# A fifteenth pair of chunks by seven products in layer 1's first MLP product, the two ordinary chunks at its head

## Chip, cores and metric

The kernel runs on one core of one Trainium2 chip. The metric is the device time of one execution in microseconds; three runs were made, and their median counts. Less is better.

## What is computed

The reference is a trunk of two layers over two sequences of 512 tokens with 1024 features, in float32. Layer 0 mixes tokens by a Fourier transform, layer 1 by attention; each is followed by the same MLP.

```python
def sq_relu_mlp(h, w_up, w_down):
    a = jnp.maximum(h @ w_up, 0)
    return (a * a) @ w_down

def trunk(x, ...):
    for i in range(DEPTH):
        ...
        x = x + sq_relu_mlp(rms_norm(x, mlp_norm[i]), mlp_w_up[i], mlp_w_down[i])
    return rms_norm(x, final_norm)
```

The inner width D_FF is 4096. The change touches the first of the two MLP products, `h @ w_up`, of layer 1.

## The kernel before

**Numbers.** Every float32 operand is split into two parts of a format that TensorE takes at full pace (`split`, L82 and L83: ScalarE casts the high part, VectorE subtracts to get the low part). A product of 128 x 128 x 512 is three matmuls.

**First product.** The 4096 columns of `w_up` are 32 chunks of 128. The operand h is cut in four blocks: its first and second half of features, for each of the two sequences (`b11`, `b21` for sequence 0, `b12`, `b22` for sequence 1). Two chunks together form a pair, and a pair is a 2 x 2 block product (chunks by sequences). It is computed by seven block products instead of eight (the scheme of Strassen and Winograd), with sums of weights (`sums_13`, `sum_2`, `sum_4`) and sums of operands (`t1` to `t4`). Each block product is `product` (L863): four blocks of 128 features, three matmuls each, so twelve matmuls of 512 columns. `Pair.first` and `Pair.second` issue two of the seven, `Pair.rest` the other five.

Layer 0 takes all 32 chunks as 16 pairs (`NPS = (16, 14)`). Layer 1 takes 14 pairs, and the chunks 28 to 31 in the ordinary way (`Regular`): per chunk and sequence two block products, 24 matmuls.

**What becomes of the results.** After the squared ReLU a pair's four results are combined by `Pair.out` (four subtractions on GpSimd, for the last pair on VectorE) and stored to DRAM (`spill`) as seven operands of the second product, which also multiplies blocks by seven products. The operands go in groups (`ROW_GROUPS`, `SUM_GROUPS`): in layer 1 the first group of `b11` and `b21` holds pairs 0 to 3, the first group of `t1`, `t3`, `t2`, `b22`, `t4` pairs 0 and 1. The results of the ordinary chunks go to `plain` in DRAM and are read at the very end of the layer, in a product with the rest of `w_down`.

**Order in layer 1, before.** `first_product` runs, in program order: `first` and `second` of the first six pairs (`AHEADS[1]` is 6), while `blocks.second()` prepares the operands of sequence 1 and the sums step by step (`next(todo)`); the four ordinary chunks for sequence 1 (L1070); `rest` of the pairs 0 to 12, with `first` of the later pairs; `rest` of pair 13; the four ordinary chunks for sequence 0 (L1119). During the last `rest` a generator, `ahead`, fetches and splits the first operands of the second product: it is resumed at three places of `rest` (L963, L970, L977), and drained after it.

**Order in layer 0.** There the last pair's `first` and `second` are issued inside the `rest` of the last but one (`early`), which frees the buffers of `b11` and `b21` sooner, and `ahead` is resumed once before that, three times in it, and three times in the last `rest`. Each resumption fetches one operand and splits the one fetched in the step before.

**Second product.** `second_product` (L1122) begins in layer 1 with one row block (`Row`, twelve matmuls per half, from `b11` and later `b21`), and between its halves and after them the five products of `Sums` with `t1`, `t3`, `t2`, `b22`, `t4`. In the first group each of these five is six matmuls. Their weights are sums again (`sum_123`, `sum_4`), made on VectorE from two loads (`w_sum`) and split (`split_12`, `split_3`, `split_4`).

**Who sets the order.** A list scheduler places the instructions on each engine by program order and readiness, also ahead of earlier ones that are not ready; each engine then executes its own list in order. Under `tc.manual_schedule(engines=...)` the instructions of the named engines keep their program order among each other. Buffers come from pools: 38 buffers of 4 KB a partition (`act`) of which the blocks of h take 28 in the first product, five for raw weights, four for split weights, eight PSUM banks. A load waits until a buffer is free. SP issues most DMAs, ScalarE's queue the stores of `b11`, `b21`, `b22` and `plain`.

Of the kernel before, what the change touches and what calls it, by code (L numbers as in the profile page):

```python
# [18 lines left out]
P = 128  # L19
D = 1024  # L20
S = 512
NSEQ = 2
# [18 lines left out]
def trunk_kernel(ctx, tc, x_in, xt_in, y_out, dcos, dsin, feat, rope, gfour, gcol, grow, gfin,  # L41
# [830 lines left out]
    def first_product(l, blocks, rows, ahead):  # L872
# [7 lines left out]

        np_, ah = NPS[l], AHEADS[l]

# [4 lines left out]
        class Pair:  # L887
# [97 lines left out]
            def out(self, b11, b12, b21, b22, eng=nc.gpsimd, queue=nc.sync):  # L985
# [7 lines left out]
                for op, x in (("b11", b11), ("b21", b21), ("b22", b22), ("t1", t[:, 0]), ("t2", t[:, 1]),  # L993
                              ("t3", b12), ("t4", t4)):
                    put(op, p, x, queue)

        class Regular:

# [7 lines left out]
            def go(self):  # L1006
                q, w, o, t = self.q, halves(self.raw), ps(), tm()
                product(o, w[0], b("b11" if q == 0 else "b12"))
                product(o, w[1], b("b21" if q == 0 else "b22"), False)
                squares(t, o)  # L1010
                nc.scalar.dma_start(plain[l][self.f - 2 * np_][:, q], t)

# [47 lines left out]
        if 2 * np_ == NF:  # L1060
            pairs[0].split_1()
            pairs[0].sum_4()
            for _ in todo:
                pass
            pairs[0].split_4()
        else:
            pairs[0].load_sums()
            next(todo)
            next(todo)
            for f in range(2 * np_, NF):  # L1070
                Regular(1, f).run()
                if f < NF - 2:
                    next(todo)
            pairs[0].sums_23()
            pairs[0].sum_4()
            pairs[0].split_23()
            next(todo)
            next(todo)
            pairs[0].split_1()
            next(todo)  # L1080
            pairs[0].split_4()
            for _ in todo:
                pass
        pairs[1].load_sums()
        last = [Regular(0, f) for f in range(2 * np_, NF)]
        ahead = ahead(last[1:])

# [8 lines left out]
        for p, pair in enumerate(pairs[:-1]):  # L1096
            if p >= ah:
                pair.first()
            with tc.manual_schedule(engines={ET.DVE}) if p <= ah else nullcontext():
                done = pair.rest(pairs[p + 1], early(ahead) if not last and p == np_ - 2 else iter(()))  # L1100
            if p + 2 < len(pairs):
                if p + 2 >= ah:
                    pairs[p + 2].load()
                pairs[p + 2].load_sums()
            elif last:
                last[0].load()
            if not last and p == np_ - 3:
                next(ahead)
            pair.out(*done, queue=nc.sync if last or p < np_ - 2 else nc.gpsimd)

        if last:
            pairs[-1].first()
        with tc.manual_schedule(engines={ET.DVE, ET.SP} | (set() if last else {ET.PE})):
            done = pairs[-1].rest(None, ahead)
        with tc.manual_schedule(engines={ET.SP}):
            for _ in ahead:
                pass
            pairs[-1].out(*done, nc.vector)
        for r in last:  # L1119
            r.go()  # L1120

    def second_product(l, blocks, rows, late=lambda split_them: None, ready=lambda m: None):  # L1122
# [129 lines left out]

        def ahead(regular):
            n = SUM_GROUPS[l][0][1]
            if not regular:
                h = fetch("b11", 0, 4)
# [27 lines left out]
                return  # L1284
            group(0, 0, ROW_GROUPS[l][0][1], (0, 1))
            regular[0].load()
            yield
            group(0, 0, ROW_GROUPS[l][0][1], (1, 2))
            regular[1].load()
            yield  # L1290
            group(1, 0, n, (0, 2))
            regular[2].load()
            yield
            group(1, 0, n, (2, 5))
            early[0, 0, 0] = row_raw(0, 0, ROW_GROUPS[l][0][1])
            for q in range(NSEQ):
                residual(q, 0)
            early[1, 0, 0] = sums_raw(0, 0, n)
            for q in range(NSEQ):
                residual(q, 1)  # L1300

# [654 lines left out]
```

## Time and profile before

| What | Value |
|---|---|
| median of 3 runs | 1694.37 us |
| lowest, highest | 1693.82, 1695.23 us |
| the profiled execution: its time | 1695.11 us |
| the profiled execution: span of its instructions | 1693.3 us |
| TensorE clock granted, mean | 0.999 |
| DMA: moved, mean rate | 265.81 MB, 157 GB/s |
| matmuls, all | 7845 |

The span runs from the first to the last instruction; the time holds in addition what lies around it (1.8 us here). In the views below, a line of the timeline gives the start of a stretch of like instructions, its length, the engine, the line of the kernel, the operation, the output and the inputs with their shapes, the count, and in brackets the idle time ahead of it with what ended it. A group of the page gives the count, the busy time, the mean duration in ns, and the idle time ahead of the group. The first matmul of layer 1's first product starts at 1057.96 us, the first of its second product at about 1370 us.

### The profile page before, as it was taken

To read this page: it belongs to the slowest core of one execution; us is meant where nothing else is said; L and a number is where in the kernel's file an instruction comes from. 1 tells how busy PE (TensorE), PEld (TensorE's weight loads), DVE (VectorE), ACT (ScalarE), POOL (GpSimd) and SP (SyncE) were. 2 spreads that over 40 slices of the span, in tenths; PEclk is the share of its full clock that TensorE was granted. 3 is DMA by queue.
4 is the path that set the end of the run, shared out by engine and by line. 5 is a ranking of instruction groups with operands and counts; after the bars stand their busy time and mean duration, and the time that the engine had idled before them with its cause. 6 is when DMAs were issued, how large, how long until landed. Compare 5 with 4: busy or idle time off the path is not lost. (4 is left out here: it accounts for less than half of the span.)

```text
span 1693.3 us, 21857 instructions
## 1 busy us (share of the span) xinstructions
PE 1681.2 (99%) x7845; PEld 1395.0 (82%) x7845; DVE 1228.0 (73%) x1808; ACT 854.3 (50%) x1489; POOL 334.9 (20%) x304
## 2 busy tenths in 40 slices
PE   9999999999999999999999999999999999999998
PEld 7987888888888888888888888888888888888887
DVE  8778776557887879876588744687655479787864
ACT  7566444446243434457787714654444544344334
POOL 1321443221000000132344303014422200000002
PEclk9999999999999999999999999999999999999999
DMA  9643555449554644610000213335544686455322
GB/s 340 167 137 126 198 187 180 156 168 388 178 209 140 224 139 172 223 50 33 26 26 1 100 61 126 110 120 193 180 143 156 224 303 236 159 210 183 133 75 100
DMA packets 103679, 265.81 MB, mean 157 GB/s; under 512 B 10177, under 2 KB 10177, under 8 KB 103570
## 3 DMA queue, kind: packets, MB, share of 16 engines
q1 hardware_dynamic: 87266, 232.43, 39.2%
q10 hardware_dynamic: 14400, 26.22, 4.1%
q0 software_dynamic: 1904, 5.77, 1.7%
q8 instruction: 61, 1.00, 0.2%
q14 instruction: 48, 0.39, 0.1%
HBM read 189.40 MB, written 73.92 MB: 156 GB/s over the span
## 5 line engine op out<-in xcount | busy, mean ns | idle before, releaser
L869 PE MATMUL ps<-u,w 128*128 128x512 f32 x4656 | 1065.4, 389 | 1.4 <-ACT u L903 0.7
L869 PEld LDWEIGHTS ps<-u,w 128*128 128x128 f32 x4656 | 872.7, 188 | 185.6 <-ACT u L903 2.7
L82 ACT CAST w<-raw 128x1024 fp32r<-128x1024 f32 (+1 forms) x224 | 217.5, 981 | 445.1 <-PE ps L869 244.5
L83 DVE TENSOR_TENSOR w<-raw,w 128x1024 fp32r<-128x1024 f32 (+1 forms) x224 | 255.6, 1144 | 60.8 <-ACT w L82 60.3
L156 POOL TENSOR_TENSOR t<-t,t 128x512 f32<-128x512 f32 (+1 forms) x56 | 77.7, 1388 | 738.3 <-ACT t L154 682.2
L82 ACT CAST u<-u 128x1024 fp32r<-128x1024 f32 (+1 forms) x131 | 131.3, 1044 | 76.0 <-PE ps L869 47.2
L83 DVE TENSOR_TENSOR u<-u,u 128x1024 fp32r<-128x1024 f32 (+1 forms) x131 | 155.3, 1211 | 19.3 <-ACT u L82 18.6
L77 PE MATMUL ps<-u,u 128*128 128x512 f32 (+2 forms) x388 | 150.2, 388 | 0.4 <-DVE u L83 0.4
L1141 DVE TENSOR_TENSOR u<-ps,u 128x512 f32<-128x512 f32 x160 | 109.4, 686 | 51.2 <-PE ps L869 48.9
L78 PE MATMUL ps<-u,u 128*128 128x512 f32 (+2 forms) x388 | 144.4, 372 | 0.4 <-DVE u L83 0.3
L79 PE MATMUL ps<-u,u 128*128 128x512 f32 (+2 forms) x388 | 144.4, 372 | 0.0
L869 PE MATMUL ps<-u,u 128*128 128x512 f32 x576 | 137.8, 390 | 0.2 <-DVE u L1141 0.2
L869 PEld LDWEIGHTS ps<-u,u 128*128 128x128 f32 x576 | 107.9, 188 | 23.8 <-DVE u L1141 0.6
L989 POOL TENSOR_TENSOR u<-u 128x512 f32<-128x512 f32 x28 | 37.2, 1329 | 398.7 <-ACT u L885 398.7
L83 DVE TENSOR_TENSOR u<-ps,u 128x512 fp32r<-128x512 f32 (+4 forms) x118 | 74.7, 649 | 19.3 <-ACT u L82 18.3
L79 PEld LDWEIGHTS ps<-u,u 128*128 128x128 f32 x388 | 73.1, 188 | 12.9
L78 PEld LDWEIGHTS ps<-u,u 128*128 128x128 f32 x388 | 73.4, 189 | 11.7 <-DVE u L83 1.3
L77 PEld LDWEIGHTS ps<-u,u 128*128 128x128 f32 x388 | 73.3, 189 | 10.7 <-DVE u L83 0.6
L82 ACT CAST u<-ps 128x512 fp32r<-128x512 f32 (+4 forms) x118 | 65.5, 562 | 26.5 <-PE ps L79 11.5
L947 DVE TENSOR_TENSOR t<-ps,u 128x512 f32<-128x512 f32 x30 | 20.7, 690 | 80.0 <-PE ps L869 57.9
L852 DVE TENSOR_TENSOR u<-ps,u 128x512 f32<-128x512 f32 (+1 forms) x48 | 30.9, 644 | 64.4 <-PE ps L79 64.4
L77 PE MATMUL ps<-u,w 128*128 128x512 f32 (+2 forms) x192 | 65.0, 338 | 0.0
(247 smaller groups left out, 1983.8 us busy)
## 6 DMA issues: line engine op xcount, KB each, us to landing
raw<-w_up SPq DMA_DIRECT2D x82, 512.0 KB, 4.5
u<-spill_t SPq DMA_DIRECT2D x60, 512.0 KB, 6.1
raw<-w_sum SPq DMA_DIRECT2D x56, 512.0 KB, 4.2
u<-spill_b SPq DMA_DIRECT2D x45, 512.0 KB, 5.6
spill_t<-u SPq DMA_DIRECT2D x87, 256.0 KB, 2.0
spill_b<-t ACTq DMA_DIRECT2D x60, 256.0 KB, 3.4
raw<-w_row SPq DMA_DIRECT2D x28, 512.0 KB, 4.0
park<-u SPq DMA_DIRECT2D x24, 512.0 KB, 3.7
```

Of the source, the lines that this page charges most:

```text
L77: nc.tensor.matmul(out, lh, rh, start=first, stop=False)
L78: nc.tensor.matmul(out, lh, rl, start=False, stop=False)
L79: nc.tensor.matmul(out, ll, rh, start=False, stop=last)
L82: nc.scalar.copy(dst_hi, src)
L83: eng.tensor_sub(dst_lo, src, f32(dst_hi))
L156: nc.gpsimd.tensor_add(acc[q][:, :n], acc[q][:, :n], s[:, :n])
L852: nc.vector.tensor_add(x[:, :n], o[:, :n], x[:, :n])
L869: nc.tensor.matmul(o, w[x][:, sl], h[k][y], start=first and k + i == 0, stop=k == n - 1 and i == 2, skip_group_check=not first)
L947: nc.vector.tensor_add(u2, ob, t[:, 0])
L989: eng.tensor_sub(t[:, 0], b12, b11)
L1141: nc.vector.tensor_add(x, o, x)
```

## The change

Layer 1 takes 15 pairs. The chunks 28 and 29 become the fifteenth pair (`NPS[l] + l`). The groups of the second product stay as they were: the fifteenth pair isn't stored as seven operands, but its four results go to `plain` as they are (`out_plain`), so it skips the sums of `Pair.out`, and the second product and the end of the layer read what they read before. The two ordinary chunks left, 30 and 31, stand at the head of the first product for both sequences, sequence 1 first, with one load and one split of their weights. At the end of the first product nothing follows the last pair. Layer 1's end is given the form of layer 0's: the last pair's first two products inside the `rest` of the last but one, `ahead` resumed seven times in smaller steps, and TensorE under the hand-written order in the last `rest`.

```diff
-        np_, ah = NPS[l], AHEADS[l]
+        np_, ah = NPS[l] + l, AHEADS[l]
...
+            def out_plain(self, b11, b12, b21, b22):
+                for i, x in enumerate(((b11, b12), (b21, b22))):
+                    for q in range(2):
+                        nc.sync.dma_start(plain[l][i][:, q], x[q])
...
             def go(self):
-                q, w, o, t = self.q, halves(self.raw), ps(), tm()
-                product(o, w[0], b("b11" if q == 0 else "b12"))
-                product(o, w[1], b("b21" if q == 0 else "b22"), False)
-                squares(t, o)
-                nc.scalar.dma_start(plain[l][self.f - 2 * np_][:, q], t)
+                w = halves(self.raw)
+                for q in self.q:
+                    o, t = ps(), tm()
+                    product(o, w[0], b("b11" if q == 0 else "b12"))
+                    product(o, w[1], b("b21" if q == 0 else "b22"), False)
+                    squares(t, o)
+                    nc.scalar.dma_start(plain[l][self.f - 2 * NPS[l]][:, q], t)
...
             for f in range(2 * np_, NF):
-                Regular(1, f).run()
-                if f < NF - 2:
-                    next(todo)
+                Regular((1, 0), f).run()
+                next(todo)
...
-        last = [Regular(0, f) for f in range(2 * np_, NF)]
-        ahead = ahead(last[1:])
+        ahead = ahead()
...
-                done = pair.rest(pairs[p + 1], early(ahead) if not last and p == np_ - 2 else iter(()))
+                done = pair.rest(pairs[p + 1], early(ahead) if p == np_ - 2 else iter(()))
             if p + 2 < len(pairs):
                 if p + 2 >= ah:
                     pairs[p + 2].load()
                 pairs[p + 2].load_sums()
-            elif last:
-                last[0].load()
-            if not last and p == np_ - 3:
+            if p == np_ - 3:
                 next(ahead)
-            pair.out(*done, queue=nc.sync if last or p < np_ - 2 else nc.gpsimd)
-
-        if last:
-            pairs[-1].first()
-        with tc.manual_schedule(engines={ET.DVE, ET.SP} | (set() if last else {ET.PE})):
+            pair.out(*done, queue=nc.sync if l or p < np_ - 2 else nc.gpsimd)
+
+        with tc.manual_schedule(engines={ET.DVE, ET.SP, ET.PE}):
             done = pairs[-1].rest(None, ahead)
         with tc.manual_schedule(engines={ET.SP}):
             for _ in ahead:
                 pass
-            pairs[-1].out(*done, nc.vector)
-        for r in last:
-            r.go()
+            if l:
+                pairs[-1].out_plain(*done)
+            else:
+                pairs[-1].out(*done, nc.vector)
...
-        def ahead(regular):
+        def ahead():
             n = SUM_GROUPS[l][0][1]
-            if not regular:
+            if l == 0:
...
-            group(0, 0, ROW_GROUPS[l][0][1], (0, 1))
-            regular[0].load()
+            h = fetch("b11", 0, 4)
             yield
-            group(0, 0, ROW_GROUPS[l][0][1], (1, 2))
-            regular[1].load()
+            put("b11", h)
+            h = fetch("b21", 0, 4)
+            raw = row_raw(0, 0, 4)
             yield
-            group(1, 0, n, (0, 2))
-            regular[2].load()
+            h1 = fetch("t1", 0, n)
+            yield
+            residual(0, 0)
+            h3 = fetch("t3", 0, n)
+            yield
+            put("b21", h)
+            rows_early[0] = halves(raw, 4 * P)
+            yield
+            put("t1", h1)
+            put("t3", h3)
+            early[1, 0, 0] = sums_raw(0, 0, n)
             yield
             group(1, 0, n, (2, 5))
-            early[0, 0, 0] = row_raw(0, 0, ROW_GROUPS[l][0][1])
-            for q in range(NSEQ):
-                residual(q, 0)
-            early[1, 0, 0] = sums_raw(0, 0, n)
-            for q in range(NSEQ):
-                residual(q, 1)
+            for m in range(2):
+                for q in range(NSEQ):
+                    residual(q, m)
```

`group(1, 0, n, (2, 5))` fetches and at once splits `t2`, `b22` and `t4`, one after the other; `residual` loads a part of the layer's input to which the second product is added; `sums_raw` loads the two raw weights of a `Sums`, `row_raw` that of a `Row`.

## The prediction

> **What bounds the kernel now.** I read the page first: span, busy shares, granted clock.
>
> ```profile
> span 1693.3 us, 21857 instructions
> PE 1681.2 (99%) x7845; PEld 1395.0 (82%) x7845; DVE 1228.0 (73%) x1808; ACT 854.3 (50%) x1489; POOL 334.9 (20%) x304
> PEclk9999999999999999999999999999999999999999
> L869 PE MATMUL ps<-u,w 128*128 128x512 f32 x4656 | 1065.4, 389 | 1.4 <-ACT u L903 0.7
> L869 PE MATMUL ps<-u,u 128*128 128x512 f32 x576 | 137.8, 390 | 0.2 <-DVE u L1141 0.2
> ```
>
> TensorE is busy 99% of the span at full clock. All matmuls of the two MLPs stand under L869: 4656 + 576 = 5232, with 1.4 + 0.2 us of idle before them. That agrees with a count in the code: 1344 + 1344 in layer 0, 1368 + 1176 in layer 1. A busy engine need not be at its peak, because a record's 389 ns overlaps the next one. So the timeline of TensorE comes next, for the pace.
>
> ```profile
> 1215.38 16.48 PE L869 MATMUL ps<-u,w 128*128 128x512 f32 x72
> 1231.70 2.88 PE L869 MATMUL ps<-u,u 128*128 128x512 f32 x12
> ```
>
> From start to start 72 matmuls take 1231.70 - 1215.38 = 16.32 us, so one takes 0.2267 us. One product of twelve takes 2.72 us. Between the stages of layer 1 this pace hardly breaks. The two places that the change touches, head and tail of the first product, are these:
>
> ```profile
> 1057.96 1.75 PE L869 MATMUL ps<-u,w 128*128 128x512 f32 x7
> 1059.87 12.37 PE L869 MATMUL ps<-u,w 128*128 128x512 f32 x53 [0.16 <-DVE u L224]
> ...
> 1072.89 5.75 PE L869 MATMUL ps<-u,w 128*128 128x512 f32 x24
> ```
>
> ```profile
> 1348.66 24.64 PE L869 MATMUL ps<-u,w 128*128 128x512 f32 x108
> 1373.33 3.29 PE L869 MATMUL ps<-u,u 128*128 128x512 f32 x12
> 1376.45 2.88 PE L869 MATMUL ps<-u,w 128*128 128x512 f32 x12
> 1379.17 8.32 PE L869 MATMUL ps<-u,u 128*128 128x512 f32 x36
> 1387.71 3.04 PE L869 MATMUL ps<-u,u 128*128 128x512 f32 x12 [0.22 <-DVE u L1141]
> 1390.59 2.88 PE L869 MATMUL ps<-u,w 128*128 128x512 f32 x12
> ```
>
> Head: seven matmuls should take 1.59 us and took 1059.87 - 1057.96 = 1.91, so 0.3 us is lost at the very start, which the change leaves alone; 24 should end after 5.60 us and took 5.75. Tail: against 2.72, 8.16 and 24.48 us the starts are late by 0.19 (1373.33), 0.40 (1376.45), 0.38 (1387.71) and 0.16 (1390.59). **The opening of the second product loses 1.13 us now.** So the bound is the number of matmuls, and whatever VectorE and the DMAs fail to prepare in time for that opening.
>
> **Part 1: fewer matmuls.** Chunks 28 and 29 cost 2 chunks x 2 sequences x 24 = 96 matmuls before; as a fifteenth pair they cost 7 x 12 = 84. Twelve go: 12 x 0.2267 = **2.72 us off TensorE**. Chunks 30 and 31 keep their 96. Nothing hides this gain: TensorE is the bound on both sides.
>
> The Trainium skill, "TensorE: Matmul & The Clock Gate", section "Wait — 56ns, not 53.3ns?", gives 215.7 ns between warm matmuls of 512 columns; by it the gain would be 2.59 us. The trace has 0.2267 us and decides.
>
> **Part 2: the head.** TensorE does 96 matmuls of ordinary chunks there before and after. Each of two weight chunks now serves both sequences, so two loads and two splits go from the busiest stretch of VectorE.
>
> ```profile
> 1100.00:1120.00 20.00, 20.00 (x90) 16.56 (x89) 18.86 (x19) 13.47 (x18) 0.00 (x0) 1.00 0.34 117
> 1220.00:1240.00 20.00, 20.00 (x90) 16.57 (x89) 10.72 (x14) 8.87 (x13) 7.25 (x7) 1.00 0.44 159
> 1400.00:1420.00 20.00, 20.00 (x90) 16.34 (x89) 19.96 (x24) 11.51 (x13) 0.00 (x0) 1.00 0.86 307
> ```
>
> The columns are TensorE, its weight loads, VectorE, ScalarE, GpSimd, clock, DMA share. VectorE has 18.86 of 20 us at the head, and TensorE still does not wait. Two splits fewer (2.3 us by the rows below) are hidden: worth 0, at most the 0.15 us above. Stores are the same number there, only four of them moved from the tail. The steady pairs (10.72 of 20 us on VectorE) are unchanged, and one more of them fits.
>
> **Part 3: the tail, the open term.** Before, 96 of the 108 matmuls in the row of 1348.66 (21.8 us) are the ordinary chunks of the first sequence, run behind the last pair's products, and the split of the second product's operands hides under them. Now TensorE goes from the last pair straight into the second product. Call the end of the last pair 0. Then b11 and the first row weight are needed at 0, t1 and its weight sum s1 at +2.72, t3 and s3 at +4.08, b21 at +5.44, t2 at +8.16, b22 at +9.5, t4 at +10.9, and the sums of the next block at +12.2. Layer 0 already ends with this hand-over, so its VectorE rows price it:
>
> ```profile
> 397.70 1.59 DVE L83 TENSOR_TENSOR w<-raw,w 128x1024 fp32r<-128x1024 f32 x1 [0.60 <-ACT w L82]
> 399.21 0.68 DVE L961 TENSOR_TENSOR t<-ps,t 128x512 f32<-128x512 f32 x1
> 399.81 2.34 DVE L83 TENSOR_TENSOR u<-u,u 128x1024 fp32r<-128x1024 f32 x2
> 402.08 1.21 DVE L83 TENSOR_TENSOR w<-raw,w 128x1024 fp32r<-128x1024 f32 x1
> 403.21 2.35 DVE L83 TENSOR_TENSOR u<-u,u 128x1024 fp32r<-128x1024 f32 x2
> 405.48 1.21 DVE L83 TENSOR_TENSOR w<-raw,w 128x1024 fp32r<-128x1024 f32 x1
> 406.62 0.68 DVE L972 TENSOR_TENSOR t<-ps,t 128x512 f32<-128x512 f32 x1
> 407.22 0.68 DVE L981 TENSOR_TENSOR u<-ps,t 128x512 f32<-128x512 f32 x1
> ```
>
> ```profile
> 401.59 2.88 PE L869 MATMUL ps<-u,u 128*128 128x512 f32 x12
> 404.31 35.98 PE L869 MATMUL ps<-u,w 128*128 128x512 f32 x158
> ```
>
> There 0 is at 404.31. The hand-ordered VectorE chain begins at 399.21 (-5.1) with the sum of the third product. A split follows each 1.14 us, an addition each 0.60. TensorE waits nowhere, but it has four row products (10.9 us) before it needs a weight sum; layer 1 has one (2.72).
>
> In layer 1 the same chain is: one addition, b21 (2 splits), the row weight (1), t1 and t3 (2), an addition, t2, b22 and t4 (3), the last addition. That is 8 x 1.14 + 3 x 0.60 = 10.9 us, from -5.1 to **+5.8**. Operands come in time: b21 at -2.2, t1 and t3 by +1.2, t2 at +3.0, b22 at +4.1, t4 at +5.3. Queued behind this chain are the weight sums, whose times are these:
>
> ```profile
> 1363.65 0.42 DVE L1208 TENSOR_TENSOR raw<-raw,raw 128x256 f32<-128x256 f32 x1 [0.98 <-DMA raw<-w_sum]
> ...
> 1373.31 1.63 DVE L83 TENSOR_TENSOR u<-raw,u 128x512 fp32r<-128x512 f32 x3 [6.29 <-ACT u L82]
> ...
> 1383.70 0.42 DVE L1208 TENSOR_TENSOR raw<-raw,raw 128x256 f32<-128x256 f32 x1 [2.11 <-DMA raw<-w_sum]
> ```
>
> s1 wants two of these 0.4 us operations, a 0.5 us cast (between them and the split, on ScalarE) and a split (a third of 1.63, 0.55): some 1.9 us, 1.4 of them on VectorE. From both sides: if they stand ahead of the chain, in VectorE's idle gaps behind the first two products (layer 0's row of 397.70 is such a split, put into the gap ahead of 399.21), s1 waits for nothing, and even the 0.59 us lost at 1373 to 1376 goes. If they stand behind it, s1 is there at +7.7 and TensorE waits 5.0 us. I take the first, because that row shows it, and because the weights' buffers come free when the last pair's weights are split (about -16).
>
> It is not free even then. From -5.1 to +12.2 VectorE has 17.3 us. It has to do the chain (10.9), the first block's weight sums (four operations and three splits, 3.2, of which s1's 1.4 ahead of the chain), five additions (3.0) and s1 of the next block (1.4): 17.1 us, so hardly any slack. In the kernel before it could afford the gaps of 6.29 and 2.11 us above. The fetches land late:
>
> ```profile
> u<-spill_t SPq DMA_DIRECT2D x60, 512.0 KB, 6.1
> u<-spill_b SPq DMA_DIRECT2D x45, 512.0 KB, 5.6
> ```
>
> t2's buffers come free at -10.9, when its product is done, so its fetch lands at about -5 and t4's, two behind, nearer 0. On SP they are queued with the four stores of pair 13, which wait for GpSimd's sums. For pair 11 (last product over at 1310.58) the stores went out like this:
>
> ```profile
> 1314.41 2.94 SPq L879 DMA_DIRECT2D spill_t<-u  x3
> 1318.28 0.32 SPq L879 DMA_DIRECT2D spill_t<-t  x1
> ```
>
> That is 3.8 to 8.0 us behind the pair; pair 13 ends at -13.6, so its stores go at -9.8 to -5.6. Fetches behind them land up to 5 us later, and the last splits slip by 1 to 2 us, a wait of TensorE of the same order. I put the opening at **1.4 us lost instead of 1.13, bounds 0 and 6.1** (5.0 + 1.1). The last pair's four plain stores replace seven stores and four subtractions; they are read only at the layer's end: 0.
>
> **Sum.** -2.72 - 0 + 0.3 = **-2.4 us**. The profiled execution took 1695.11 us (1.8 around its span); it lies 0.74 above the median of 1694.37. So 1692.7 for such an execution, **1692.0 as a median**. A measurement of this kernel tells 0.2% (3.4 us) from no change; the gain is under that.
>
> **Rivals.**
> 1. *Forecast: small waits.* 0.3 to 2.5 us lost in the opening: -3.55 to -1.35, 1690.8 to 1693.0. Chance 0.55.
> 2. *A cleaner opening and head.* All 1.13 us of the opening go, and 0.15 at the head: -2.72 - 1.13 - 0.15 = -4.0, 1690.4. For it: s1 early, and less VectorE work at the head. Against: no slack on VectorE. Chance 0.11.
> 3. *Weight sums partly behind the chain.* TensorE waits 2.5 to 5 us in all, the gain is eaten: 1693.0 to 1695.5. For it: the chain's operations come earlier in the program, and s1 needs a buffer that the fetches want too. Chance 0.24.
> 4. *Slower: s1 behind the whole chain, in its place at +5.8.* 5.0 us of wait and the later 0.54: -2.72 + 5.54 - 1.13 = +1.7, 1696.1. It decides from 3.85 us lost in the opening (2.72 + 1.13). With t2's fetch queued behind pair 13's stores (2 us more) it comes to +3.7, 1698.1. For it: every operation of the chain is earlier in the program. Against: layer 0's row of 397.70. Chance 0.10, of which 0.06 over 0.2%.
>
> The Trainium skill, the same page, section "What's actually happening", lets an idle window of about 3.4 us halve TensorE's clock. In rival 4 alone TensorE would stand that long; the next 3.4 us at half pace would add up to 1.7 us, an estimate from that page, giving 1697.8 instead of 1696.1. No row here has such a gap: clock 1.00 in all windows shown.
>
> That the change saves no matmuls at all cannot be; the counts are fixed by the code.
>
> **Range and chances.** 1690.4 to 1696.2 leaves out the better half of rival 2 and the worse half of rival 4. Faster by over 0.2% (under 1690.98): rival 2 and the forecast's edge, 0.14. Slower by over 0.2%: 0.06. The rest, 0.80.
>
> **What would show it.** L869 with 5220 matmuls instead of 5232, and the first product shorter by 2.72 us. After the last pair a first product from `w`, then `u` products: any start later than 2.72 us after it measures s1's wait, and its releaser names VectorE or ScalarE. VectorE's operations of L1208 ahead of the last L961 confirm part 3; behind L981 they refute it. Wrong altogether if waits appear in the steady pairs or at the head.

## The result, and the profile after

The changed kernel takes **1699.62 us** (median of 7 runs, 1699.11 to 1700.03), the kernel before in the same comparison 1694.58 (7 runs, 1693.82 to 1695.23): ratio 1.0028, 95% interval 1.0018 to 1.0038. It is 5.0 us slower; the prediction said 2.4 us faster, with 1696.2 as the end of its range. The profiled executions took 1699.23 and 1695.11 us, so between the two traces 4.1 us are to be found.

The page of the kernel after:

```profile
span 1697.5 us, 21830 instructions
PE 1680.0 (99%) x7833; PEld 1394.8 (82%) x7833; DVE 1229.0 (72%) x1811; ACT 853.6 (50%) x1488; POOL 339.5 (20%) x308
L869 PE MATMUL ps<-u,w 128*128 128x512 f32 x4632 | 1060.3, 390 | 2.3 <-DVE w L83 1.3
L869 PE MATMUL ps<-u,u 128*128 128x512 f32 x588 | 141.9, 393 | 4.9 <-ACT u L82 4.9
```

4632 + 588 = 5220 matmuls of the MLPs, twelve fewer, as the change says. The idle time ahead of them went from 1.6 to 7.2 us, 4.9 of it in front of matmuls with operands and weights in `u` buffers, put down to ScalarE's cast at L82. TensorE's timeline after, at the end of layer 1's first product and through the opening of the second:

```profile
1367.48 2.88 PE L869 MATMUL ps<-u,w 128*128 128x512 f32 x12
1375.23 4.84 PE L869 MATMUL ps<-u,u 128*128 128x512 f32 x12 [4.87 <-ACT u L82]
1379.91 2.88 PE L869 MATMUL ps<-u,w 128*128 128x512 f32 x12
1382.63 11.04 PE L869 MATMUL ps<-u,u 128*128 128x512 f32 x48
...
1412.55 6.05 PE L869 MATMUL ps<-u,w 128*128 128x512 f32 x26
1419.43 30.90 PE L869 MATMUL ps<-u,w 128*128 128x512 f32 x135 [0.83 <-DVE w L83]
```

The first product now starts at 1057.60 (before 1057.96) and the second at 1367.48 (before 1370.43), so the first product is 309.88 instead of 312.47 us long: the 2.6 us are there. They are lost three times over behind it.

- **A wait.** The product with t1 and the weight sum s1 should start 2.72 us after the first row, at 1370.20. It starts at 1375.23, 5.03 us late.
- **Slow matmuls behind the wait.** The twelve matmuls from there on (six with s1, six with s3) take until 1379.91, 4.68 us instead of 2.72: 1.96 us more.
- **A second wait.** From 1412.55 to 1419.43 there are 6.88 us for 26 matmuls (5.89): 0.99 us. This is in the second group of operands, 40 us further on.

Together 7.98 us against 1.13 before, so 6.85 more, less 2.72 for the twelve matmuls: +4.13, and the spans differ by 1697.5 - 1693.3 = 4.2. In the kernel before, TensorE ran into the second group without a wait:

```profile
1409.63 30.68 PE L869 MATMUL ps<-u,w 128*128 128x512 f32 x134
```

The slow matmuls have their reason in the clock. Windows after (TensorE, weight loads, VectorE, ScalarE, GpSimd, then granted clock, DMA share and GB/s):

```profile
1370.00:1375.00 5.00, 0.36 (x2) 0.00 (x0) 3.30 (x4) 3.01 (x5) 0.00 (x0) 0.73 0.85 326
1375.00:1379.00 4.00, 3.77 (x9) 2.96 (x10) 3.72 (x9) 2.68 (x7) 0.00 (x0) 0.50 0.64 208
```

In the second window the clock is 0.50: nine matmuls in 4 us. The Trainium skill, "TensorE: Matmul & The Clock Gate", section "What's actually happening", says that an idle window of about 3.4 us sends the array to half rate until it has been busy for as long; the trace agrees, with 5.03 us of standing still and 1.96 us lost after it (the prediction's estimate from that page was up to 1.7). That shorter waits can do it as well is seen in e_fill below.

Why did s1 come late? VectorE after, from the first weight sums to s1's split:

```profile
1352.68 0.42 DVE L1210 TENSOR_TENSOR raw<-raw,raw 128x256 f32<-128x256 f32 x1
...
1355.03 0.41 DVE L1218 TENSOR_TENSOR raw<-raw,raw 128x256 f32<-128x256 f32 x1
...
1362.24 0.69 DVE L961 TENSOR_TENSOR t<-ps,t 128x512 f32<-128x512 f32 x1 [1.97 <-PE ps L869]
...
1373.33 0.68 DVE L981 TENSOR_TENSOR u<-ps,t 128x512 f32<-128x512 f32 x1
1375.21 0.69 DVE L83 TENSOR_TENSOR u<-raw,u 128x512 fp32r<-128x512 f32 x1 [1.20 <-ACT u L82]
```

The weight sums (L1210 to L1218) are made ten microseconds ahead of the chain (L961 to L981), where there was idle time. The split that follows them, at 1375.21, stands behind the whole chain. It is a split into a `u` buffer (`u<-raw,u`), and ScalarE casts for it at the same late place:

```profile
1374.04 0.63 ACT L884 ACTIVATE u<-u 128x512 f32<-128x512 f32 x1 [1.89 <-DVE u L981]
1374.58 0.60 ACT L82 CAST u<-raw 128x512 fp32r<-128x512 f32 x1
```

In the compiled program that cast waits for GpSimd and for two DMAs: its buffer was one of those that held pair 13's results. GpSimd subtracts them until 1361.7, and SP stores them at 1357.84 to 1361.72. Such stores land 2.0 to 2.2 us after their issue here (medians), so the buffer was free by about 1364. The cast comes ten microseconds later because it stands in ScalarE's list behind L884 at 1374.04, and L884 waits for L981, the end of the chain. So the first theory was that **the missing buffer** made the scheduler put the split behind the chain; the rivals were the clock, the missing cover at the tail, and VectorE's load.

### The profile page after: what moved, and what is told of

The parts are those of the page before. It is cut to its first block, busy times and chain, and to the rows that moved or that the text cites. A ratio compares the mean times of both kernels' runs of the same rounds, so it can differ in the third digit from the quotient of the medians.

```text
span 1697.5 us, 21830 instructions
## 1 busy us (share of the span) xinstructions
PE 1680.0 (99%) x7833; PEld 1394.8 (82%) x7833; DVE 1229.0 (72%) x1811; ACT 853.6 (50%) x1488; POOL 339.5 (20%) x308
## 5 line engine op out<-in xcount | busy, mean ns | idle before, releaser
L82 ACT CAST w<-raw 128x1024 fp32r<-128x1024 f32 (+1 forms) x221 | 214.5, 981 | 451.5 <-PE ps L869 260.8
L83 DVE TENSOR_TENSOR w<-raw,w 128x1024 fp32r<-128x1024 f32 (+1 forms) x221 | 252.0, 1143 | 63.1 <-ACT w L82 62.4
L82 ACT CAST u<-u 128x1024 fp32r<-128x1024 f32 (+1 forms) x131 | 131.0, 1044 | 68.5 <-PE ps L869 45.3
L1143 DVE TENSOR_TENSOR u<-ps,u 128x512 f32<-128x512 f32 x160 | 109.5, 686 | 56.7 <-PE ps L869 54.0
L869 PE MATMUL ps<-u,u 128*128 128x512 f32 x588 | 141.9, 393 | 4.9 <-ACT u L82 4.9
L869 PEld LDWEIGHTS ps<-u,u 128*128 128x128 f32 x588 | 111.6, 190 | 28.7 <-ACT u L82 5.3
L79 PEld LDWEIGHTS ps<-u,u 128*128 128x128 f32 x388 | 73.1, 188 | 13.0
L77 PEld LDWEIGHTS ps<-u,u 128*128 128x128 f32 x388 | 73.3, 189 | 10.7 <-DVE u L83 0.6
L78 PEld LDWEIGHTS ps<-u,u 128*128 128x128 f32 x388 | 73.4, 189 | 10.5
L82 ACT CAST u<-ps 128x512 fp32r<-128x512 f32 (+4 forms) x118 | 65.5, 561 | 26.9 <-PE ps L79 11.6
```

The lines of the kernel that those rows point to most:

```text
L77: nc.tensor.matmul(out, lh, rh, start=first, stop=False)
L78: nc.tensor.matmul(out, lh, rl, start=False, stop=False)
L79: nc.tensor.matmul(out, ll, rh, start=False, stop=last)
L82: nc.scalar.copy(dst_hi, src)
L83: eng.tensor_sub(dst_lo, src, f32(dst_hi))
L869: nc.tensor.matmul(o, w[x][:, sl], h[k][y], start=first and k + i == 0, stop=k == n - 1 and i == 2, skip_group_check=not first)
```

## The experiments

Every kernel was timed in 3 or 5 rounds beside the kernel before, whose medians were 1694.74 to 1694.99 us in the five comparisons. Two waits are followed in the kernels of the table, worked out from TensorE's timeline. **A** is the time from the first row of the second product to its second group of operands, less 168 matmuls (38.08 us). **B** is the time lost in the first 26 matmuls of that second group. **Lead** is the time from VectorE's first weight sum for the second group to TensorE's arrival there. All three are taken from the one profiled execution, which can lie 1.3 us from the median (e_own3: 1697.28 against 1698.60). Slow matmuls behind the second wait are not in B. A sum or an addition stands some lines lower in kernels with lines put in (L1210 as L1216 or L1219, L1143 as L1146).

| Kernel | median, us | ratio to before (95%) | A | B | lead |
|---|---|---|---|---|---|
| before | 1694.58 | 1 | 1.1 | 0 | 11.2 |
| after | 1699.62 | 1.0028 (1.0018 to 1.0038) | 7.0 | 1.0 | 10.1 |
| e_own3 | 1698.60 | 1.0020 (1.0012 to 1.0029) | 1.3 | 4.3 | 4.6 |
| e_skip_a | 1698.01 | 1.0020 (1.0011 to 1.0029) | 0 | 4.1 | 4.6 |
| e_skip_b | 1692.49 | 0.9987 (0.9978 to 0.9996) | 1.3 | 0 | 4.6 |
| e_plain | 1699.12 | 1.0025 (1.0015 to 1.0035) | 7.7 | 0 | 12.6 |
| e_plain13 | 1696.99 | 1.0010 (1.0001 to 1.0019) | 4.9 | 1.0 | 10.1 |
| e_plain_own | 1695.55 | 1.0006 (0.9997 to 1.0014) | 1.3 | 2.8 | 7.4 |
| e_plain13_own | 1696.09 | 1.0009 (1.0000 to 1.0018) | 3.1 | 1.0 | 10.1 |
| e_swap | 1691.27 | 0.9979 (0.9970 to 0.9988) | 0.2 | 0 | 7.1 |
| e_swap13 | 1690.70 | 0.9975 (0.9966 to 0.9985) | 0 | 0 | 9.6 |

### The buffer alone: e_own3

The first sums of layer 1 put their split weights into the pool of split weights (`own`), not into buffers that the results held.

```diff
+            def home(self):
+                return narrow if self.n == 2 and (l, self.m, self.g) != (1, 0, 0) else own
...
-                self.s2, self.s1 = halves(self.s, self.n * P, (own, narrow)[self.n == 2])
+                self.s2, self.s1 = halves(self.s, self.n * P, self.home())
```

(the same for s4 and for s3 with a22)

> The changed kernel, but the split weights of the first Sums of layer 1 (s1, s2, s3, the second half of s3's load, s4) are put into the pool of split weights instead of the pool of operands. Theory 'buffer': s1's sum is ready some 14 us early, and only its split waits, for a buffer that pair 13's results hold. Then the 4.87 us wait ahead of the first product with s1 goes to under 0.5 us, the clock stays at 1.00, and the time falls by about 7 us, from 1699.6 to 1692.4 (1691.7 to 1693.2). Rival 'chain': VectorE and ScalarE are too full in the last 11 us, whatever the buffer; then 3 us or more of wait stay, and the time is 1696 to 1700.

Measured: 1698.60 us (1696.45 to 1699.81). TensorE's timeline:

```profile
1367.99 4.69 PE L869 MATMUL ps<-u,w 128*128 128x512 f32 x20
1373.66 8.00 PE L869 MATMUL ps<-u,w 128*128 128x512 f32 x34 [0.98 <-DVE w L83]
...
1407.34 3.33 PE L869 MATMUL ps<-u,w 128*128 128x512 f32 x14
...
1417.49 2.79 PE L869 MATMUL ps<-u,w 128*128 128x512 f32 x11 [1.92 <-DVE w L83]
```

s1's wait and the slow matmuls behind it are gone: the row product and the first product of sums now run on as one stretch from 1367.99. So the choice of the buffer was the cause of that wait. But the time hardly follows. TensorE comes to the second group 5.2 us earlier (1407.34 for 1412.55) and waits there for 4.3 us. Half the theory holds; what holds the second group had to be found.

### The clock alone: e_fill

Twenty matmuls into an unused PSUM bank are put between the first row and the first product of sums.

```diff
+                if l and k == 0:
+                    warm(20, b["b11"][0][0])
```

> The changed kernel with twenty more matmuls of 512 columns, whose result nobody reads, between the first row product and the product with s1, where TensorE waits 4.87 us. Theory 'clock': the nine matmuls at 0.427 us behind the wait are slow because the wait halved the clock; with 20 x 0.2267 = 4.5 us of the wait filled, the clock stays at 1.00 and some 2 us go: 1697.5 (1697.0 to 1698.2). Rival: they are slow because their operands come late; then the time stays at 1699.6 or rises.

Measured: 1700.49 us (1699.33 to 1701.18), ratio 1.0033 (1.0021 to 1.0045). TensorE's timeline:

```profile
1370.56 4.69 PE L356 MATMUL ps<-u 128*128 128x512 f32 x20
1375.63 3.32 PE L869 MATMUL ps<-u,u 128*128 128x512 f32 x12 [0.38 <-ACT u L82]
1378.79 2.89 PE L869 MATMUL ps<-u,w 128*128 128x512 f32 x12
...
1419.90 5.40 PE L869 MATMUL ps<-u,w 128*128 128x512 f32 x16 [2.41 <-DVE w L83]
```

The twelve matmuls behind the gap go from start to start in 1378.79 - 1375.63 = 3.16 us, not 4.68 (2.72 at full pace), so the clock explains most of the slow ones. The time saved turns up again as 2.4 us of waiting at 1417 to 1420: the same second group as in e_own3. The 16 matmuls behind that wait take 5.4 us instead of 3.8, at a granted clock of 0.50 between 1420 and 1422, so the time ends above the expected 1697.5. A wait of 2.41 us was thus followed by half clock here, and one of 2.72 us in e_plain13_own was not (1.00 in all windows around it): these traces show no single length of a wait that decides it.

### The cover: e_14pairs and e_tail

e_14pairs keeps 14 pairs and puts all four ordinary chunks at the head: no fifteenth pair, but also nothing behind the last one.

```diff
-        np_, ah = NPS[l] + l, AHEADS[l]
+        np_, ah = NPS[l], AHEADS[l]
```

> The changed kernel with 14 pairs: all four ordinary chunks stand at the head for both sequences, the last pair is stored as seven operands. Only the arrangement of head and tail is left of the change. Theory 'cover': the tail without ordinary products makes the wait, the number of pairs has no part in it: the wait of about 5 us and the halved clock stay, and the 12 matmuls are back: 1702.3 (1701 to 1704). Rival 'pair': the fifteenth pair with its buffers makes the wait; then the time is near the kernel before, 1693.5 to 1695.5.

Measured: 1704.99 us (1704.45 to 1706.42), ratio 1.0061 (1.0047 to 1.0075), 1 us above the expected range.

```profile
1370.18 2.88 PE L869 MATMUL ps<-u,w 128*128 128x512 f32 x12
1379.61 5.27 PE L869 MATMUL ps<-u,u 128*128 128x512 f32 x12 [6.55 <-ACT u L82]
```

The wait is there without the fifteenth pair: 6.7 us from 1372.90 to 1379.61. It belongs to the tail's arrangement. e_tail gives half of the cover back: the two ordinary chunks run for sequence 1 at the head and for sequence 0 behind the last pair.

```diff
-                Regular((1, 0), f).run()
+                Regular((1,), f).run()
...
+        for f in range(2 * np_, NF):
+            Regular((0,), f).run()
```

> The changed kernel, but the two ordinary chunks are computed at the head for sequence 1 alone and behind the last pair for sequence 0, as in the kernel before: 48 matmuls, 10.9 us of cover. Theory 'cover' (and 'buffer' with it): s1 is split within these 10.9 us, the wait is under 1 us, the clock stays at 1.00: 1691.9 (1691.2 to 1693.0), below both kernels. Rival: the smaller steps of the operands or the hand-written order themselves make the wait; then over 3 us of it stay, 1695 to 1700.

Measured: 1700.64 us (1698.85 to 1701.37), ratio 1.0033 (1.0021 to 1.0045). That is in the rival's direction, but not for its reason: the tail loses only 2.1 us, 0.2 of it in front of s1 and nothing at the second group. But the head, with 48 fewer matmuls, loses 7.1 us in new waits:

```profile
1106.42 0.51 PE L869 MATMUL ps<-u,w 128*128 128x512 f32 x1 [1.50 <-ACT u L82]
...
1118.60 2.98 PE L869 MATMUL ps<-u,w 128*128 128x512 f32 x12 [3.36 <-DVE t L951]
```

The ordinary chunks are cover at both ends; there are not enough for both.

### VectorE relieved through GpSimd: e_gp_a, e_gp_b, e_gp_ab, e_gp_only

If VectorE's load holds the second group, some of its subtractions done elsewhere should free it. In e_own3, GpSimd takes the low parts of the first group's t2, b22 and t4 (a), of the second halves of the second group's operands (b), or both; e_gp_only does both without e_own3's buffers.

```diff
-                put(op, h)
+                put(op, h, (nc.vector, nc.gpsimd if (l, g) == (1, 1) else nc.vector))
```

(the edit of b; a passes GpSimd in the same way for t2, b22 and t4 of the first group)

> e_own3 with the low parts of t2, b22 and t4 of the first group (three subtractions of 128x1024, 3.4 us on VectorE) made on GpSimd, which stands idle there. Theory 'debt': VectorE comes out of the last pair some 7 us behind and TensorE pays for it wherever VectorE's lead ends (1.2 us behind the first row product, 4.1 us at 1410 to 1417 in e_own3); with 3.4 us off VectorE the waits fall from 5.4 to about 2 us: 1695.2 (1694 to 1696.5). Rival 'DMA': the waits at 1410 to 1417 come of the saturated DMAs there, not of VectorE's queue; then 4 us of them stay: 1697.5 to 1699.

> e_own3 with the second half of the low parts of the second group's five sums operands (five subtractions of 128x1024, 5.7 us on VectorE, between 1404 and 1422) made on GpSimd. Theory 'debt': VectorE's queue is what ends last at 1410 to 1417, so those 4.1 us go nearly all, and the 1.2 us behind the first row product stay: 1694.7 (1693.5 to 1696). Rival 'DMA': 1697.5 to 1699, as e_own3.

> Both: e_own3 with all eight of these subtractions on GpSimd. Theory 'debt': 9.1 us of VectorE's work go, more than the debt, so TensorE waits under 1.5 us in all from the end of the last pair to 1430, the 12 matmuls saved come through, and the time falls below both kernels: 1692.8 (1692 to 1694.2) where before has 1694.8. Rival 'DMA': 1697 to 1699.

> The changed kernel with the same eight subtractions on GpSimd, and s1's split in the pool of operands as the change has it. Theory 'debt' with 'buffer': the last addition stands earlier on VectorE, but s1's split still takes the buffer that pair 13's results leave, so TensorE waits 2 to 4 us ahead of the product with s1, and nothing at 1410 to 1417: 1696 (1694.5 to 1698). If the buffer has no part: 1692 to 1693.5, as e_gp_ab.

Measured: 1701.43 (1699.76 to 1702.54), 1698.36 (1697.09 to 1699.06), 1700.17 (1699.07 to 1701.86) and 1705.78 us (1703.6 to 1706.57). None helps: none is faster than e_own3 beyond the intervals. What works against it is seen in e_gp_b, GpSimd first and VectorE second:

```profile
1402.38 2.40 POOL L83 TENSOR_TENSOR u<-u,u 128x1024 fp32r<-128x1024 f32 x1 [40.33 <-ACT u L82]
1407.22 2.70 POOL L83 TENSOR_TENSOR u<-u,u 128x1024 fp32r<-128x1024 f32 x1 [2.44 <-ACT u L82]
```

```profile
1402.59 2.73 DVE L1216 TENSOR_TENSOR raw<-raw,raw 128x512 f32<-128x512 f32 x1
1405.25 0.68 DVE L1143 TENSOR_TENSOR u<-ps,u 128x512 f32<-128x512 f32 x1
1406.98 0.68 DVE L1217 TENSOR_TENSOR raw<-raw,raw 128x512 f32<-128x512 f32 x1
1407.69 2.77 DVE L1218 TENSOR_TENSOR raw<-raw,raw 128x512 f32<-128x512 f32 x1
```

A weight sum that takes 0.68 us takes 2.73 and 2.77 when a GpSimd subtraction runs. So GpSimd gives VectorE one split (1.14 us) and takes 2 us from it. These four runs do not tell whether VectorE's load is the cause.

### VectorE relieved by leaving work out: e_skip_b and e_skip_a

Here nothing else does the work: in e_own3 the low parts of the second halves of the second group's operands (b), or of the first group's t2, b22 and t4 (a), are not computed.

```diff
-                put(op, h)
+                put(op, h, (1,) if (l, g) == (1, 1) and op in SUM else ())
```

(the edit of b; a does the same for t2, b22 and t4 of the first group)

> As e_own3, but the low parts of the second halves of the next group's five sum operands are not computed (five subtractions of 128x1024, 5.7 us of VectorE, left out of the stretch of 1405 to 1425 us; the operands are then not split there, so the output is not the reference's). No other engine takes them over. VectorE's lag: the 4.4 us that TensorE waits at 1410 to 1417 fall under 1 us, and the time to 1694 to 1695.5. A late transfer: the waits at 1410 to 1417 stay at 3.5 to 5 us and the time at 1698 to 1699.

> As e_own3, but the low parts of the first group's t2, b22 and t4 are not computed (three subtractions of 128x1024, 3.4 us of VectorE, out of the chain behind the last pair; the output is not the reference's). VectorE's lag: the opening's 1.25 us go, and of the 4.4 us at 1410 to 1417 some 3.4 go as well, because whatever VectorE is spared at the start it is ahead later: 1694 to 1696. If instead the later waits belong to transfers or buffers of the next group, only the 1.25 us go: 1697 to 1698.

Measured: e_skip_b 1692.49 us (1691.64 to 1693.32), e_skip_a 1698.01 (1696.61 to 1699.63). In e_skip_b TensorE runs through the second group without a wait:

```profile
1373.96 8.01 PE L869 MATMUL ps<-u,w 128*128 128x512 f32 x34 [0.98 <-DVE w L83]
...
1407.64 22.64 PE L869 MATMUL ps<-u,w 128*128 128x512 f32 x99
```

So the wait at the second group is VectorE's work of that very stretch. e_skip_a refutes the simple reading, that a lag is carried on: 3.4 us spared 35 us earlier take away the opening's 1.3 us and leave 4.1 of the 4.3 behind it. (The median falls by 0.6 us only; in this trace the clock is 0.50 from 1416 to 1420, behind the second wait.) VectorE could not use them:

```profile
1375.77 0.69 DVE L1146 TENSOR_TENSOR u<-ps,u 128x512 f32<-128x512 f32 x1 [4.04 <-PE ps L869]
...
1385.26 0.42 DVE L1219 TENSOR_TENSOR raw<-raw,raw 128x256 f32<-128x256 f32 x1 [1.75 <-DMA raw<-w_sum]
```

It stood idle for 4.04 us, and for 1.75 us at the next block's sums, whose weights had not been loaded. The second group is a burst that can only begin when its weights are there; with the work and its order as they are, B falls as the lead grows (4.3 us at a lead of 4.6, 0 at 11.2 before). So what held up the loads?

### The rows first: e_rows

The changed kernel with layer 1's four row blocks of the first group ahead of the first block of sums, as in layer 0, so that s1 is due 8.2 us later.

```diff
-        steps = [(... if l or i else 16 * g - 8 + 4 * m if g else m - 4, i, m, g, n)
+        steps = [(... if i or l and g else 16 * g - 8 + 4 * m if g else m - 4, i, m, g, n)
```

> The changed kernel with the four row blocks of layer 1's first group put ahead of the first block by sums, as layer 0 has them. The first weight sum s1 is then due 10.9 us behind the last pair's end and not 2.72; the first results of rows are taken over by ScalarE's copies, so VectorE has some 8 us in which it only splits. VectorE's lag and the missing buffer: both are covered, the waits at 1370 and the slow matmuls go, and little is lost at 1410 to 1417 (the row blocks move work of VectorE from there to behind the opening, 0 to 3 us): 1691.5 to 1695. If the lag only moves (three blocks by sums of 6.8 us each then stand without rows between them, each with about 6.2 us of VectorE), 3 to 6 us of waits appear between 1385 and 1410 and the time stays at 1696 to 1699.

Measured: 1702.10 us (1700.24 to 1702.70), slower than either expectation. The opening loses 1.9 us; the second group loses 8.2 us, slow matmuls at half clock among them. Its loads of `w_sum` go out from 1403.73 on, VectorE's first sum for it stands at 1410.88, and the product with s1 starts at 1418.80. In the other kernels a row product of 2.72 us comes ahead of that one, so by the table's measure the lead is 5.2 us, nearly as short as in e_own3. TensorE goes on at 1426.18 and 1427.89, when the cast (1426.13) and the subtraction (1427.84) of s3's split end. Cover moved to the opening seems to be cover taken from the second group; this was not tried on its own.

### The queue: e_plain and e_plain_own, e_plain13 and e_plain13_own

SP's timeline in e_own3 shows what stands ahead of the weight loads:

```profile
1368.81 1.56 SPq L1155 DMA_DIRECT2D u<-park  x3
1377.53 0.32 SPq L1000 DMA_DIRECT2D plain<-u  x1
1377.90 0.92 SPq L1000 DMA_DIRECT2D plain<-t  x2
1378.87 1.06 SPq L1155 DMA_DIRECT2D u<-park  x2
1380.02 2.67 SPq L91 DMA_DIRECT2D raw<-w_sum  x4
```

From 1370.37 on SP does nothing until it can store the last pair's result, which ScalarE squares until 1377.51 (L885). The waits of SP's queue between 1365 and 1382, with total, number and longest:

```profile
SPq L1000 <- ACT u L82: 7.4, 1, 7.4
```

(The view names the cast that stands ahead of L885 in ScalarE's list.) Behind the stores are the weights of the next blocks. The edit sends these four stores (`out_plain`) over ScalarE's queue, and in the two kernels with 13 also gives pair 13's seven stores the queues of layer 0.

```diff
-                        nc.sync.dma_start(plain[l][i][:, q], x[q])
+                        nc.scalar.dma_start(plain[l][i][:, q], x[q])
...
-            pair.out(*done, queue=nc.sync if l or p < np_ - 2 else nc.gpsimd)
+            pair.out(*done, queue=nc.sync if p < np_ - 2 else nc.gpsimd)
```

(the second edit in the two with 13 only)

> As e_own3, but the last pair's four plain stores go out on ScalarE's queue, as the stores of the ordinary chunks do, and not on SP's. Held-up loads: the second block's weight loads, issued at 1380.0 us in e_own3, go out 5 to 8 us earlier, VectorE's idle time for them goes, the 4.4 us of waits at 1410 to 1417 fall to 0 to 2 us, and the time to 1693 to 1696. VectorE's load alone: loads earlier, waits the same, 1698 to 1699.

> The changed kernel with the four plain stores on ScalarE's queue; the first sums keep their buffers, so s1's split still waits for pair 13's results. Held-up loads: the 5.0 us and the slow matmuls at 1370 stay (7 us), the 1.1 us at 1418 go: 1697.5 to 1699. If the plain stores have no part in it: 1699.6 as before this edit.

> As e_plain_own, and pair 13's seven stores on GpSimd's and ScalarE's queues as in layer 0, off SP's. t2's fetch, issued at 1362.6 us behind these stores in e_own3, goes out some 5 us earlier. If late operands have a part in the opening's 1.25 us, that falls under 0.5 and the time is 0.5 to 1.5 us under e_plain_own; if VectorE's chain alone makes it, the same time as e_plain_own within 0.5 us.

> The changed kernel with both groups of stores off SP's queue, buffers as they are. s1's split waits for the buffers of pair 13's results, which come free when the stores from them are done: stores on GpSimd's queue need not be earlier. Missing buffer: the wait at 1370 stays at 3 to 5 us, 1696 to 1699. If SP's queue alone had held s1: wait under 1.5 us, 1693 to 1695.

Measured: e_plain_own 1695.55 us (1694.54 to 1697.68), 3 us under e_own3 by the medians and 1.5 us by the waits of the two traces; e_plain 1699.12 (1698.84 to 1700.18); e_plain13_own 1696.09 (1694.72 to 1698.75); e_plain13 1696.99 (1696.00 to 1697.23). In e_plain_own the first of the weight loads goes out 6.5 us earlier:

```profile
1373.56 0.33 SPq L91 DMA_DIRECT2D raw<-w_sum  x1
```

and the lead grows from 4.6 to 7.4 us while B falls from 4.3 to 2.8 (0 to 2 was expected). The other three of these loads follow from 1379.43 on, hardly earlier than before; how the lead comes of it was not followed load by load. e_plain has its lead of 12.6 us and no wait at the second group, but keeps the missing buffer's 7.7 us at the opening: two causes, one at each place. In time it is not told apart from the changed kernel. e_plain13_own fetches t2 at 1357.20 instead of 1362.53 and gains nothing by it (1696.09 against 1695.55), so the opening's last 1.3 us are not late operands. With the operands earlier, all three of their splits stand ahead of s3's split at 1374.81, and the opening loses 3.1 us, as much more as B loses less. e_plain13 shows a second way to shorten s1's wait without another buffer: with pair 13's stores off SP it is 2.4 us at first, and 0.8 more in front of the third matmul, which needs a low part; 1.7 more go to half clock behind them (0.50 from 1375 to 1377).

### The order of the splits: e_swap, e_swap13, e_before_swap

What is left in e_plain_own, VectorE and TensorE:

```profile
1372.81 0.68 DVE L83 TENSOR_TENSOR w<-raw,w 128x512 fp32r<-128x512 f32 x1
...
1414.64 1.22 DVE L83 TENSOR_TENSOR w<-raw,w 128x1024 fp32r<-128x1024 f32 x1
```

```profile
1373.55 8.04 PE L869 MATMUL ps<-u,w 128*128 128x512 f32 x34 [0.98 <-DVE w L83]
...
1415.91 24.32 PE L869 MATMUL ps<-u,w 128*128 128x512 f32 x106 [2.58 <-DVE w L83]
```

Both times TensorE goes on when the split of s3 ends (1373.49 and 1415.86). s3 is due second of the five products, s4 fourth, and the code splits s4 first.

```diff
             sums.split_12()
+            sums.split_3()
             sums.sum_4()
             sums.split_4()
-            sums.split_3()
...
-                    sums.split_3()
+                    sums.split_4() if l else sums.split_3()
...
-                        nsums.split_4()
+                        nsums.split_3() if l else nsums.split_4()
```

> As e_plain_own, but in layer 1's second product s3's weights are split ahead of s4's (s3 is due second of the five, s4 fourth). Order as the cause: the waits of 1.25 us at 1372 and 2.85 us at 1413 fall under 1 us together, time 1691.5 to 1693, under the kernel before by 0.1 to 0.2%. VectorE's load as the cause: the waits come back in front of s4 or t2 with 2 to 4 us, 1694.5 to 1696.

> As e_plain13_own with the same exchange; its waits are 3.0 us at 1372 and 1.1 us at 1415, both in front of s3. Order: both under 1 us together, 1691.5 to 1693.5. Load: 1695 to 1697.

> The kernel before with the same exchange in layer 1, nothing else: it loses 1.1 us in the opening in all, so the exchange can give at most that: 1693.7 to 1695, no difference that can be told.

Measured: e_swap 1691.27 us (1690.88 to 1691.93), e_swap13 1690.70 (1690.22 to 1691.47), the control e_before_swap 1694.07 (1693.65 to 1694.99), ratio 0.9996 (0.9987 to 1.0005). TensorE in e_swap13:

```profile
1367.69 12.40 PE L869 MATMUL ps<-u,w 128*128 128x512 f32 x54
1379.93 6.96 PE L869 MATMUL ps<-u,u 128*128 128x512 f32 x30
...
1405.77 19.43 PE L869 MATMUL ps<-u,w 128*128 128x512 f32 x85
```

From 1367.69 to 1405.77 are 38.08 us, 168 matmuls at full pace, and no wait behind. The split of s3 in the opening now stands at 1360.99, ahead of the chain. **Both versions beat the kernel before and the kernel after.** Against the control, which has the exchange and no fifteenth pair, e_swap13 is 3.4 us faster: about the 2.72 us of the twelve matmuls and the 0.9 us that the control still loses in its opening. e_swap and e_swap13 are not told apart by their intervals. No kernel has the exchange without the moved stores, so whether these are still needed is not shown.

## Why the prediction was wrong

**Part 1 was right.** Twelve matmuls fewer, 2.6 us off the first product (2.72 predicted). e_swap13 shows that it is worth its full size once nothing waits.

**Part 2 was right.** Next to nothing new is lost at the head: 2.59 of the 2.72 us come through. e_tail adds why: with 48 fewer matmuls there, 7.1 us are lost.

**Part 3 failed, in the step "If they stand ahead of the chain, in VectorE's idle gaps ... I take the first".** The reason given was that "the weights' buffers come free when the last pair's weights are split (about -16)". The sums did stand ahead of the chain, at 1352.68 to 1355.44. But s1's split doesn't use the weights' buffers: sums of two pairs go to the same `u` buffers as the operands, and the one it got had held pair 13's results. The split came out behind the chain. That is the wait of rival 4, which had a chance of 0.10; its 5.0 us were measured as 5.03. But rival 4 gave the program order as its reason, and the sums were not held back by that; a buffer that s1 lacks was named in rival 3. So the price was right and its reason was not. The prediction's sign for part 3, the sums (L1208) ahead of the last L961, came out as if part 3 were confirmed: it watched the sums and not the split. The term of the opening, "1.4 us lost instead of 1.13, bounds 0 and 6.1", measured 7.0 us, and 1.0 more at the second group, for which the sum had no term. Layer 0's row of 397.70, the reason for the choice, is a split into a `w` buffer, and so no evidence for this one. e_own3 shows the step: another buffer, and the wait of 5.03 us is gone.

**The chain's length was nearly right.** It was to run from -5.1 to +5.8; it ran from 1362.24 to 1374.01, which is -5.2 to +6.5 from 1367.48, with 0.7 us of waiting for ScalarE in it.

**The clock was right for this gap**: the measured loss was 1.96 us where the estimate had up to 1.7. With it rival 4 came to 1697.8; the measured 1699.62 lies 1.8 us above that, 0.99 of it by the second wait, for which no rival had a term.

**"Hardly any slack" was right and not followed to its end.** The sum of VectorE's work was made up to +12.2. The price was paid beyond that too, at +45: 1.0 us in the changed kernel and, once s1's wait is taken away, 4.3 us at the second group. Three things are named by the runs. The last pair's four plain stores, priced at 0 because "they are read only at the layer's end", stand on SP's queue ahead of weight loads and held them up (e_plain_own against e_own3: 3 us by the medians, 1.5 us by the traces). The work of the second group on VectorE is a burst with too short a lead (e_skip_b: gone with five splits fewer). And within the burst s3 is split behind s4 (e_swap against e_plain_own: 4.3 us). In the kernel before, 21.8 us of ordinary products and a lead of 11.2 us covered all three. The prediction looked for who reads the stores, and not for who is queued behind them.

What is left open: why B is 1.0 us with a lead of 10.1 and 0 with one of 11.2 was not taken apart operation by operation. e_own3's executions spread over 3.4 us, and this goes with the mean granted clock: the three at 0.999 took 1696.45 to 1697.28 us, the eight at 0.997 or 0.998 took 1698.05 to 1699.81, and 0.001 of the span is 1.7 us. The profiled one is among the three and keeps a clock of 1.00 behind its second wait, where the trace of e_skip_a, with nearly the same wait, has 0.50. So the second wait probably halved the clock in most executions of e_own3; no trace here shows such an execution.

## What to carry to other kernels

Work that only fills TensorE at a seam between stages is also time for the loads and splits of the next stage; before it is taken away, list for each operand there its buffer's last user, its place in the DMA queue and its place on the engine, and not just the engine's total. A store that nobody reads soon still costs what is queued behind it, so put it on the queue of the engine that makes its data. And when one wait is removed and the time stays, look for the next place where the same engine's lead runs out: three small faults of 1 to 5 us hid a gain of 2.7.

## What the runs showed of the hardware that was not expected

A GpSimd subtraction of two SBUF operands of 128x1024 (2.4 to 2.7 us) stretched VectorE's sum of two SBUF operands from 0.68 to 2.77 us; VectorE's addition with one operand in PSUM stayed at 0.68 (those at 1420.13 and 1423.47, while GpSimd was busy from 1416.37 to 1425.81). The Trainium skill, "SBUF — State Buffer", section "SBUF: two separate sides", says that such a VectorE operation and a GpSimd operation that reads SBUF exclude each other for a whole instruction; the rows of e_gp_b agree: the sums at 1402.59 and 1407.69 end with or after the GpSimd operations begun at 1402.38 and 1407.22.
